# Half of the attention keys projected by seven-product blocks, in the stage of the queries

## The chip, the cores and the metric

The kernel runs on one core of a Trainium2 chip. The metric is the device time of one execution in microseconds (us). PE is the matrix engine, DVE the vector engine, ACT the scalar engine, POOL the general engine, SP the engine that issues most DMAs.

## What is computed

One decoder block over 1024 tokens of width 1024 in float32: an RMSNorm with a modulation gives `h`; one wide projection of `h` gives the operands of a retention branch, of an attention branch and two gates; their sum goes through an output projection, and an MLP follows. The change lies in the attention branch:

```python
proj = h @ w_in                                   # split into parts
for gi, (win, dil) in enumerate(ATT_GROUPS):      # (128,1), (512,4), (2048,16)
    aq, ak, av = parts[4 + 3 * gi], parts[5 + 3 * gi], parts[6 + 3 * gi]
    o, lse = dilated_group(heads(aq, 4), heads(ak, 4), heads(av, 4), tab, win, dil)
# in dilated_group, per head and block of a strided subsequence:
s = q @ k.T * dh ** -0.5 + bias ; mx = max(s) ; e = exp(s - mx) ; o = (e / sum(e)) @ v
```

There are three groups of four heads with 128 channels each, so twelve queries, twelve keys and twelve values. The three groups' outputs of a head are weighted by a softmax over their denominators.

## The kernel before, in words

**Numbers.** Every operand of a matmul is split into a high half (a rounded copy, made by ACT) and a low half (the rest, made by a DVE subtraction). `mm3` (L215) then issues three matmuls, low x high, high x low and high x high, at L219, L221 and L223.

**Stages.** In order: start-up and the first values, the remaining values of attention (`av_blocks`), queries and keys (`queries_keys`, L1186), the values of retention, 32 chunks of retention, attention in two passes (`pair` 0 and 1, each with two heads of each of the three groups), the output of both branches, the MLP.

**Projections of two kinds.** A plain projection of 128 columns is `proj_gen` (L508): eight pieces over the contraction, each six matmuls of 512 columns, so 48. It wants its weights split (`wsplit`, `split_w`). The other kind takes two 128-column projections at once as a 2 x 2 block product done by seven products instead of eight (class `Blocks`): each product has 4 x 3 matmuls, so 84 matmuls for what two plain projections do in 96. The seven products are listed in `ORDER`; `prep` makes DVE's sums of weight blocks and the two halves, `post` combines results on DVE and ACT, and `a_out` (L1136) puts them into token order and stores them to DRAM. `PAIRS` (L1110) lists what the stage `queries_keys` makes in this way: eight pairs of retention's queries and keys ("r"), four of its gates ("s"), six of attention's queries ("a"), four of the output gates ("g"): 22 pairs. Weights of pair q+2 are fetched at the start of pair q, 512 KB twice.

**Attention.** `combos` lists the six heads of a pass in the order group 1, group 1, group 2, group 2, group 0, group 0. `att_step(pair, i)` (L1769) does the plain projection of key i, woven with the scores of head i-1: `weave` puts the scores' matmuls between the eight pieces, the first of them after three pieces (`lag=2`). Step 0 has no scores; in pass 0 it ends the retention and in pass 1 it runs beside the PV part of pass 0. `cover_step(pair, 0)` (L1809) does the same with the projection of an output gate and the scores of head 5. `cover_step(pair, 1)` projects another gate while the softmax ends. From `cover_step(pair, 2)` on, transposes (L1653) and PV products run, woven with further gates.

Of a head i, PE makes the scores bank by bank (three banks for group 1, two for group 2, four for group 0; PSUM has four such banks for them). DVE adds the bias from PSUM into `P` (L1508, L1512), `k_split` (L1473) makes the next key's halves from PSUM (ACT L1477, DVE L1478), `scores_end` (L1515) takes row maxima on DVE (L1518 to L1526), negates them (L1528) and has ACT do eight exponentials (L1531). After head 5, `weights` (L1601) makes the softmax over groups and `pscale` (L1632) scales the probabilities.

**Order.** Engines get their instructions in the order of the program. `Steps.run` (L71) decides where the preparation of a step's operands stands: ahead of a step's body it calls `prepare` for the next step, and for the one after that as far as its first weight:

```python
for t in (s + 1, s + 2):
    ...
        prepare(t, room - done, t == s + 2)
...
body(*args)
```

The operands come through three raw tiles of 512 KB. Whenever one is prepared, the load of the operand three places later is issued on SP. `q_prep` (L1464) makes a query's halves: ACT L1468, DVE L1469; `split_w` a weight's: ACT L209, DVE L210.

Of the kernel before, what the change touches and what calls it, by code (L numbers as in the profile page):

```python
# [11 lines left out]
F32 = mybir.dt.float32  # L12
# [5 lines left out]
P = 128  # L18
D = 1024
S = 1024  # L20
NK = D // P
H = 4
# [111 lines left out]
def block_kernel(ctx, tc, io, stop=None, dbg=None):  # L134
# [25 lines left out]
    def ps_mm(name):  # L160
        return PS["first"].pop("mm", None) or PS["p"].tile([P, 2, 512], F32, tag="mm", bufs=PS["mm"], name=name)
# [346 lines left out]
    def proj_gen(ps, w):  # L508
        for k in range(NK):
            proj_mm(ps, w, [k])  # L510
            yield
# [334 lines left out]
    def wsplit(ap):  # L846
        return ap, split_w


    va_d = [dram.tile([S, 512], F32, name=f"vad{g}") for g in range(3)]  # L850
    aq_d = {(p, g, a): dram.tile([P, S], F32, name=f"aqd{p}{g}{a}") for p in range(2) for g in range(3) for a in range(2)}
    h12_d = [dram.tile([P, 2, 512], F32, name=f"h12d{m}") for m in range(4)]
    av = {}

# [252 lines left out]
    a_pairs = [("a", g, p) for p in range(2) for g in range(3)]  # L1107
    g_pairs = [("g", i) for i in range(len(GATES) // 2)]
    s_pairs = [("s", h) for h in range(H)]
    PAIRS = [{"r": r_pairs, "a": a_pairs, "g": g_pairs, "s": s_pairs}[i].pop(0) for i in "rsrarsrarsrarsraggagga"]  # L1110
    NA = len(PAIRS)
    OA = {}

    def a_load(q, part):
        pair = PAIRS[q]
        src = io[{"g": "w_gate2", "a": "w_aq", "s": "w_rg2"}.get(pair[0]) or f"w_r{pair[1]}"]
        i = 2 * pair[1] + pair[2] if pair[0] == "a" else pair[-1]
        if q == 0 or q % 2 == 0 and part == 2:
            r = x4(f"wa{q}{part}")
        else:  # L1120
            r = wraw.tile([P, 1024], F32, tag="raw", name=f"wa{q}{part}")
        nc.sync.dma_start(r, src[2 * i + part - 1])
        BA.raw[q, part] = r
# [12 lines left out]
    def a_out(q, n, x, y=None):  # L1136

        pair = PAIRS[q]
        if q not in OA:
            OA[q] = [x4(f"qa{q}{i}") for i in range(2)]  # L1140
        i, t = int(n[0]) - 1, int(n[1]) - 1
        o, view = OA[q][i][:, 512 * t:512 * t + 512], lambda z: z
        if pair[0] == "a" and pair[1] == 1:
            o = OA[q][i].rearrange("p (r n i) -> p r n i", r=4, n=2)[:, :, t, :]
            view = lambda z: z.rearrange("p (i r) -> p r i", r=4)
        elif pair[0] == "a" and pair[1] == 2:
            o = OA[q][i].rearrange("p (r i) -> p r i", r=8)[:, :, 64 * t:64 * t + 64]
            view = lambda z: z.rearrange("p (i r) -> p r i", r=8)
        f = {"g": AF.Sigmoid, "s": AF.Silu}.get(pair[0], AF.Copy)
        if y is None:  # L1150
            nc.scalar.activation(o, view(x), f)
        else:
            (nc.vector.tensor_add if n == "12" else nc.vector.tensor_sub)(o, view(x), view(y))
            if pair[0] in "gs":
                nc.scalar.activation(o, o, f)
        if n in ("12", "21"):
            if pair[0] == "g":
                dst = gate_d[GATES[2 * pair[1] + i]]
            elif pair[0] == "s":
                dst = srg_d[pair[1]][i]  # L1160
            elif pair[0] == "a":
                dst = aq_d[pair[2], pair[1], i]
            else:
                return
            nc.sync.dma_start(dst, OA[q][i])
# [203 lines left out]
    steps.add(av_blocks, manual=True)  # L1369
    steps.add(queries_keys, manual=True)  # L1370

    r_loads = {(0, 0): [io["w_rg"][0]], (H - 1, 7): [io["w_ak"][4]]}
    for t in range(1, 2 * H):
        r_loads[(t // 2, 2) if t % 2 else (t // 2 - 1, 7)] = [io["w_rg"][t]]

# [88 lines left out]
    def q_prep(pair, g, a):  # L1464

        def prep(raw):
            hi, lo = ring(f"qh{pair}{g}{a}"), ring(f"ql{pair}{g}{a}")
            nc.scalar.mul(hi, raw, QSCALE)  # L1468
            nc.vector.scalar_tensor_tensor(lo, raw, QSCALE, fv(hi), op0=ALU.mult, op1=ALU.subtract)  # L1469
            A["q", g, a] = (hi, lo)  # L1470
        return prep

    def k_split(pair, g, a, ps):  # L1473
# [76 lines left out]
    def v_fetch(pair, g):  # L1550

        for j in range(2):
            lo = A["l", g, j] = v_tile(pair, g, j, "vl")
            nc.sync.dma_start(fv(lo).rearrange("p (a b) -> p a b", a=4), v_rows(pair, g, j))
# [211 lines left out]

    combos = [(g, a) for g in (1, 2, 0) for a in range(2)]

    def att_step(pair, i):  # L1769

        g, a = combos[i]

        def body(*args):
            ps = ps_mm(f"ak{pair}{i}")
            gen = proj_gen(ps, hd.pop("w") if i == pair == 0 else args[-1])
            if i == len(combos) - 2:
                v_fetch(pair, 0)
            if i > 0:
                last = combos[i - 1]
                weave(gen, NK, scores_gen(pair, *last), len(SB[last[0]]), lag=2)  # L1780
            elif pair == 0:
                args[0](1, True)
                for _ in range(4):
                    next(gen)
                on_T(H - 1, NC - 2)
                on_T(H - 1, NC - 1)
                drain(gen)
                u_final(H - 1)
                for add in result_sums(slice(4, 8)):
                    add()  # L1790
                open_att()
                args[0](3)
            else:
                weave_pv(gen, NK, 0, 10, args[0], lambda: k_split(pair, g, a, ps))
            if i == 0:
                A["st"] = A["p"].tile([P, 3, 8, 4], F32, tag="st", name=f"st{pair}")
                bias_load(pair)
            later_loads()
            if i == 0 and pair == 1:
                banks_sc()  # L1800
            else:
                k_split(pair, g, a, ps)
            if i > 0:
                scores_end(pair, *last)
                if last[1] == 1:
                    stats_out(pair, last[0])
        return body

    def cover_step(pair, n):  # L1809


        i = COVER[pair][n]

        def body(*args):
            if n == 2:
                banks_pv((("mm", "ac2", "ac3", "s", "ac0", "ac1"), ("ac0", "ac1", "s", "ac2", "ac3", "mm"))[pair])
                v_fetch(pair, 2)
            ps = ps_mm(f"gate0{i}")
            gen = proj_gen(ps, args[-1])
            if n == 0:  # L1820
                v_fetch(pair, 1)
                weave(gen, 6, scores_gen(pair, *combos[-1]), len(SB[0]), lag=2, rest=False)
                drain(gen)
                later_loads()
                for j in range(2):
                    vs_high(pair, 0, j)
                t = ring(f"g0{i}s", F32)
                nc.scalar.copy(t, flat(ps))
                A["gate", 0] = t, t
                scores_end(pair, *combos[-1])  # L1830
                weights(pair)
                pscale(0, 0)
            elif n == 1:
                drain(gen)
                t = ring(f"g0{i}s", F32)
                nc.vector.tensor_copy(t, flat(ps))
                A["gate", 1] = t, t
            else:
                weave_pv(gen, NK, pair, 20 if pair else (16, 14)[n - 2], args[0])
                t = A["r1"].tile([P, S], F32, tag="att", bufs=8, name=f"g0{i}s")  # L1840
                nc.scalar.activation(t, flat(ps), AF.Sigmoid)
                nc.sync.dma_start(gate_d[i], t)
        return body

    for pair in range(2):
        for i, (g, a) in enumerate(combos):
            steps.add(att_step(pair, i),
                      ([] if i == pair == 0 else [wsplit(io["w_ak"][g * 4 + 2 * pair + a])]) +
                      ([(aq_d[pair, *combos[i - 1]], q_prep(pair, *combos[i - 1]))] if i > 0 else []),
                      manual=i == 0)  # L1850
        for n in range(len(COVER[pair])):
            more = [(aq_d[pair, *combos[-1]], q_prep(pair, *combos[-1]))] if n == 0 else []
            steps.add(cover_step(pair, n), more + [wsplit(io["w_gate"][len(COVER[0]) * pair + n])], manual=n > 0)


    G = {}
# [779 lines left out]
def _cols(w):  # L2636

    k, n = w.shape
    return np.ascontiguousarray(w.reshape(k // P, P, n // P, P).transpose(2, 1, 0, 3)).reshape(n // P, P, -1)
# [74 lines left out]
def pack(x, c, w_ada, b_ada, norm1_g, w_in, rel_bias, ret_gn_g, ret_gn_b,  # L2714
         w_ret_out, w_att_out, w_o, norm2_g, w_ff1, w_ff2, norm_f_g):
    A = np.asarray
    w = A(w_in)[0]
    att = w[:, 6144:10752].reshape(1024, 3, 3, 512)
    rg = w[:, 4096:6144].reshape(1024, 4, 512)
    gates = lambda js: np.concatenate([w[:, 10752 + P * j:10752 + P * j + P] for j in js], axis=1)  # L2720
    a = {
# [11 lines left out]
        "w_rg": _cols(rg[:, :, :256].reshape(1024, 1024)),  # L2733
        "w_rg2": _pairs(rg[:, :, 256:].reshape(1024, 1024)),
        "w_aq": _pairs(att[:, :, 0].reshape(1024, 1536)),
        "w_ak": _cols(att[:, :, 1].reshape(1024, 1536)),
        "w_av": _vcols(att[:, :, 2].reshape(1024, 1536), 512),
        "w_gate": _cols(gates(i for c in COVER for i in c)),
        "w_gate2": _pairs(gates(GATES)),
# [26 lines left out]
```

## Time and profile before

| | us |
|---|---|
| median of 3 runs | 2184.3 (2184.2 to 2186.07) |
| the profiled execution | 2182.82 |
| its span | 2181.1 |
| PE busy | 2147.4 |
| DVE busy | 1479.0 |
| ACT busy | 947.1 |

The stage of queries lies at about 150 to 570 us of the span, attention's scores of pass 0 at 954 to 1037 us, those of pass 1 at 1107 to 1190 us. In a timeline a row has the start, the duration, the engine, the line, the operation, the output and inputs, and, where the engine idled before, for how long and what ended it. `x3` merges three neighbours.

### The profile page before, as it was taken

What the parts mean: (1) busy time and instruction counts of PE and PEld (TensorE: products, weight loads), DVE (VectorE), ACT (ScalarE), POOL (GpSimd) and SP (SyncE); (2) the same over time, 40 slices, a digit from 0 to 9 for tenths busy, and PEclk for the clock granted to TensorE, in tenths of its full rate; (3) what the DMA queues carried; (4) which work ended last, traced back from release to release, by engine and by line L of the source; (5) the groups of instructions that cost most, each with busy time, mean ns of one, the idle gap of its engine ahead of it and who ended that gap; (6) DMA issues with size and microseconds to landing.
All of it is one profiled execution on the core that took longest, in us unless ns stands there. A gap on an engine that the chain in (4) does not pass through costs nothing.

```text
span 2181.1 us, 27045 instructions
## 1 busy us (share of the span) xinstructions
PE 2147.4 (98%) x10034; PEld 1784.6 (82%) x10034; DVE 1479.0 (68%) x2281; ACT 947.1 (43%) x1715; POOL 178.4 (8%) x192
## 2 busy tenths in 40 slices
PE   7999999999999999999999999999999999999998
PEld 5888888888888888888888888888878888788887
DVE  6756777767566678854655644677876665887855
ACT  4533322333334566654644525434554455433412
POOL 0101111100000334410000000001000000000003
PEclk9999999999999999999999999999999999999999
DMA  9869998734687758977323366653054445645322
GB/s 382 231 193 297 289 328 266 217 136 155 223 297 287 257 181 242 263 222 186 105 81 108 98 250 210 224 184 130 35 202 159 154 143 188 240 138 173 109 87 78
DMA packets 161891, 422.55 MB, mean 194 GB/s; under 512 B 27734, under 2 KB 55645, under 8 KB 157662
## 3 DMA queue, kind: packets, MB, share of 16 engines
q1 hardware_dynamic: 151902, 372.57, 48.4%
q0 software_dynamic: 9856, 48.24, 10.1%
q8 instruction: 79, 1.29, 0.2%
q14 instruction: 54, 0.44, 0.1%
HBM read 325.71 MB, written 160.32 MB: 223 GB/s over the span
## 4 chain that ended last, share of the span: by engine, by line
PE 90%; DVE 4%; ACT 2%; DMA 1%; issue 1%; POOL 0%; SPq 0%; POOLq 0%; DVEq 0%; ACTq 0%
PE qap L219 6%; PE qap L223 6%; PE qap L221 6%; PE fp L219 4%; PE fp L223 4%; PE fp L221 4%; PE ak L219 2%; PE ak L221 2%; PE ak L223 2%; PE f2a L221 2%; PE f2a L223 2%; PE f2a L219 2%; PE rg L221 1%; PE rg L219 1%; PE rg L223 1%; PE va L221 1%
## 5 line engine op out<-in xcount | busy, mean ns | idle before, releaser
L219 PE MATMUL qap<-hh,qaw 128*128 128x512 f32 x264 | 102.8, 389 | 0.1
L221 PE MATMUL qap<-hl,qaw 128*128 128x512 f32 x264 | 102.7, 389 | 0.0
L223 PE MATMUL qap<-hh,qaw 128*128 128x512 f32 x264 | 102.7, 389 | 0.0
L656 POOL TENSOR_TENSOR j<-qk,j 128x512 fp32r<-128x512 f32 x32 | 48.3, 1513 | 311.7 <-ACT j L655 311.7
L2117 POOL TENSOR_TENSOR accnf<-accnf,sqnf 128x256 f32<-128x256 f32 (+1 forms) x18 | 16.6, 921 | 613.2 <-ACT sqnf L2116 613.2
L2221 ACT ACTIVATE a<-a 128x512 f32<-128x512 f32 x48 | 30.3, 632 | 78.0 <-DVE a L2220 78.0
L219 PEld LDWEIGHTS qap<-hh,qaw 128*128 128x128 f32 x264 | 49.6, 188 | 10.8 <-DVE qat L310 0.5
L221 PEld LDWEIGHTS qap<-hl,qaw 128*128 128x128 f32 x264 | 49.5, 188 | 10.3
L223 PEld LDWEIGHTS qap<-hh,qaw 128*128 128x128 f32 x264 | 49.6, 188 | 10.3
L2410 ACT CAST w2h<-w2s 128x512 fp32r<-128x512 f32 x36 | 22.4, 621 | 78.2 <-DVE w2s L2448 78.2
L2117 POOL TENSOR_TENSOR accn<-accn,sqn 128x512 f32<-128x512 f32 x12 | 15.5, 1294 | 496.0 <-ACT sqn L2116 496.0
L276 DVE TENSOR_TENSOR fw<-w1r,fw 128x512 fp32r<-128x512 f32 x48 | 32.9, 688 | 33.2 <-ACT fw L266 33.2
L1531 ACT ACTIVATE P<-P,ng 128x128 f32<-128x128 f32 (+1 forms) x96 | 41.9, 438 | 29.5 <-DVE ng L1528 29.5
L276 DVE TENSOR_TENSOR qaw<-wa,qaw 128x512 fp32r<-128x512 f32 x66 | 45.0, 686 | 11.1 <-ACT qaw L266 11.1
L1309 DVE SCALAR_TENSOR_TENSOR cossin<-cossin,cb 128x1024 f32<-128x1024 f32 x32 | 39.0, 1220 | 16.4 <-DMA cossin<-in_w_ada_dram 16.4
L219 PE MATMUL fp<-h2h,fw 128*128 128x512 f32 x128 | 50.0, 390 | 0.0
L1955 DVE TENSOR_TENSOR rwl<-rwl,rwh 128x1024 fp32r<-128x1024 f32 x25 | 30.2, 1221 | 29.0 <-ACT rwh L1985 29.0
L221 PE MATMUL fp<-h2l,fw 128*128 128x512 f32 x128 | 49.8, 389 | 0.0
L223 PE MATMUL fp<-h2h,fw 128*128 128x512 f32 x128 | 49.8, 389 | 0.0
L219 PE MATMUL roa<-rh,rwl 128*128 128x512 f32 x128 | 49.8, 389 | 0.0
L221 PE MATMUL roa<-rl,rwh 128*128 128x512 f32 x128 | 49.8, 389 | 0.0
L223 PE MATMUL roa<-rh,rwh 128*128 128x512 f32 x128 | 49.8, 389 | 0.0
(3093 smaller groups left out, 7138.1 us busy)
## 6 DMA issues: line engine op xcount, KB each, us to landing
cossin<-in_w_ada_dram SPq DMA_DIRECT2D x32, 512.0 KB, 5.3
v<-vd SPq DMA_DIRECT2D x32, 512.0 KB, 5.7
w1r<-in_w_ff_dram SPq DMA_DIRECT2D x32, 512.0 KB, 4.8
vd<-vo SPq DMA_DIRECT2D x24, 512.0 KB, 6.3
xsd<-as SPq DMA_DIRECT2D x24, 512.0 KB, 2.8
w2r<-in_w_ff2s_dram SPq DMA_DIRECT2D x24, 512.0 KB, 7.6
em<-in_w_ada_dram SPq DMA_DIRECT2D x16, 512.0 KB, 10.2
wrvs<-in_w_rv_dram POOLq DMA_DIRECT2D x16, 512.0 KB, 11.1
```

The costliest lines, as they stand in the source:

```text
L219: nc.tensor.matmul(o, wl, xh, start=first, stop=False, skip_group_check=skip)
L221: nc.tensor.matmul(o, wh, xl, start=False, stop=False, skip_group_check=skip)
L223: nc.tensor.matmul(o, wh, xh, start=False, stop=last, skip_group_check=skip)
L276: nc.vector.tensor_sub(t[:, 512:], src, fv(t[:, :512]))
L656: nc.gpsimd.tensor_sub(t[:, 1], src, fv(t[:, 0]))
L1309: nc.vector.scalar_tensor_tensor(t, t, 1.0, cb, op0=ALU.mult, op1=ALU.mult, accum_out=mods[:, j:j + 1])
L1531: nc.scalar.activation(v, v, AF.Exp, bias=ng[:, blk:blk + 1], accum_out=st[:, g, blk, 2 + a:3 + a])
L1955: nc.vector.tensor_sub(lo, fv(lo), fv(hi))
L2117: (nc.vector if f == 7 else nc.gpsimd).tensor_add(G["acc", key], G["acc", key], sq)
L2221: nc.scalar.activation(o, o, AF.Relu)
L2410: nc.scalar.copy(hi, src)
```

## The change

In each group, the keys of the second head of each pass (six of twelve) are no longer projected in attention. Three new pairs "k", one for each group, are added to `PAIRS`, which has 25 then; `a_out` orders them by token as it does queries, and stores them to `ak_d` in DRAM. In attention they are read back by `k_prep` like a query. The six other keys keep their plain projections: one is now spread over two heads' scores, four pieces to each, with the first scores after two pieces (`lag=1`). The step of head 5's gate is cut into two steps in the same way ("s" and 0). What the body of a step does after its scores, and `Steps.run`, are as before.

```diff
-    PAIRS = [{"r": r_pairs, "a": a_pairs, "g": g_pairs, "s": s_pairs}[i].pop(0) for i in "rsrarsrarsrarsraggagga"]
+    k_pairs = [("k", g) for g in range(3)]
+    PAIRS = [{"r": r_pairs, "a": a_pairs, "g": g_pairs, "s": s_pairs, "k": k_pairs}[i].pop(0)
+             for i in "rsrarsrarsrarsrakggakggak"]
...
+            elif pair[0] == "k":
+                dst = ak_d[i, pair[1]]
...
+    def k_prep(pair, g, a):
+
+        def prep(raw):
+            hi, lo = ring(f"kh{pair}{g}{a}"), ring(f"kl{pair}{g}{a}")
+            nc.scalar.copy(hi, raw)
+            nc.vector.tensor_sub(lo, raw, fv(hi))
+            A["k", g, a] = (hi, lo)
+        return prep
...
+    def weave_scores(pair, i):
+
+        weave(itertools.islice(A["gen"], NK // 2), NK // 2, scores_gen(pair, *combos[i]), len(SB[combos[i][0]]), lag=1)
+
+    def scored(pair, i):
+        scores_end(pair, *combos[i])
+        if combos[i][1] == 1:
+            stats_out(pair, combos[i][0])
+
+    def att_step(pair, i):
+
+        g, a = combos[i + 2 - i % 2]
+
+        def body(*args):
+            if i % 2 == 0:
+                A["ps"] = ps_mm(f"ak{pair}{i}")
+                A["gen"] = proj_gen(A["ps"], args[-1])
+            if i == 2:
+                v_fetch(pair, 0)
+            weave_scores(pair, i)
+            later_loads()
+            if i % 2:
+                drain(A["gen"])
+                k_split(pair, g, a, A["ps"])
+            scored(pair, i)
+        return body
...
+    def rows_load(pair, i):
+        c = combos[i]
+        k = [(ak_d[pair, c[0]], k_prep(pair, *c))] if c[1] else []
+        return k + [(aq_d[pair, *c], q_prep(pair, *c))]
...
+        steps.add(att_first(pair), k_load(combos[0][0], pair) if pair else [], manual=True)
+        for i in range(len(combos) - 2):
+            steps.add(att_step(pair, i), (k_load(combos[i + 2][0], pair) if i % 2 == 0 else []) + rows_load(pair, i))
+        for n in ("s", *range(len(COVER[pair]))):
+            more = rows_load(pair, len(combos) - 2 + (n == 0)) if n in ("s", 0) else []
+            w = [wsplit(io["w_gate"][len(COVER[0]) * pair + (0 if n == "s" else n)])] if n != 0 else []
+            steps.add(cover_step(pair, n), w + more, manual=n not in ("s", 0))
```

`att_first` is the old step 0 under a new name.

More of the change, by code (lines that the diff above doesn't have):

```diff
@@ L851, in block_kernel @@
     aq_d = {(p, g, a): dram.tile([P, S], F32, name=f"aqd{p}{g}{a}") for p in range(2) for g in range(3) for a in range(2)}
+    ak_d = {(p, g): dram.tile([P, S], F32, name=f"akd{p}{g}") for p in range(2) for g in range(3)}
     h12_d = [dram.tile([P, 2, 512], F32, name=f"h12d{m}") for m in range(4)]
@@ L1115, in a_load @@
         pair = PAIRS[q]
-        src = io[{"g": "w_gate2", "a": "w_aq", "s": "w_rg2"}.get(pair[0]) or f"w_r{pair[1]}"]
+        src = io[{"g": "w_gate2", "a": "w_aq", "k": "w_ak2", "s": "w_rg2"}.get(pair[0]) or f"w_r{pair[1]}"]
         i = 2 * pair[1] + pair[2] if pair[0] == "a" else pair[-1]
@@ L1142, in a_out @@
         o, view = OA[q][i][:, 512 * t:512 * t + 512], lambda z: z
-        if pair[0] == "a" and pair[1] == 1:
+        if pair[0] in "ak" and pair[1] == 1:
             o = OA[q][i].rearrange("p (r n i) -> p r n i", r=4, n=2)[:, :, t, :]
             view = lambda z: z.rearrange("p (i r) -> p r i", r=4)
-        elif pair[0] == "a" and pair[1] == 2:
+        elif pair[0] in "ak" and pair[1] == 2:
             o = OA[q][i].rearrange("p (r i) -> p r i", r=8)[:, :, 64 * t:64 * t + 64]
@@ L1370, in block_kernel @@
     steps.add(queries_keys, manual=True)
-    r_loads = {(0, 0): [io["w_rg"][0]], (H - 1, 7): [io["w_ak"][4]]}
+    r_loads = {(0, 0): [io["w_rg"][0]], (H - 1, 7): [io["w_ak"][2]]}
     for t in range(1, 2 * H):
@@ L1767, in block_kernel, with att_first @@
     combos = [(g, a) for g in (1, 2, 0) for a in range(2)]
-    def att_step(pair, i):
-        g, a = combos[i]
+    def att_first(pair):
+        g, a = combos[0]
         def body(*args):
[L1774 to L1781, printed above, removed]
+            ps = ps_mm(f"ak{pair}0")
+            gen = proj_gen(ps, args[-1] if pair else hd.pop("w"))
+            if pair == 0:
                 args[0](1, True)
@@ L1794, in body @@
                 weave_pv(gen, NK, 0, 10, args[0], lambda: k_split(pair, g, a, ps))
-            if i == 0:
-                A["st"] = A["p"].tile([P, 3, 8, 4], F32, tag="st", name=f"st{pair}")
-                bias_load(pair)
+            A["st"] = A["p"].tile([P, 3, 8, 4], F32, tag="st", name=f"st{pair}")
+            bias_load(pair)
             later_loads()
-            if i == 0 and pair == 1:
+            if pair == 1:
                 banks_sc()
@@ L1802, in body @@
                 k_split(pair, g, a, ps)
[L1803 to L1806, printed above, removed]
+        return body
[19 more added lines that the diff above has]
+            scored(pair, i)
         return body
     def cover_step(pair, n):
-        i = COVER[pair][n]
+        i = COVER[pair][n if n != "s" else 0]
         def body(*args):
+            if n == "s":
+                A["ps"] = ps_mm(f"gate0{i}")
+                A["gen"] = proj_gen(A["ps"], args[-1])
+                weave_scores(pair, len(combos) - 2)
+                later_loads()
+                scored(pair, len(combos) - 2)
+                return
             if n == 2:
@@ L1817, in body @@
                 v_fetch(pair, 2)
-            ps = ps_mm(f"gate0{i}")
-            gen = proj_gen(ps, args[-1])
+            ps = A["ps"] if n == 0 else ps_mm(f"gate0{i}")
+            gen = A["gen"] if n == 0 else proj_gen(ps, args[-1])
             if n == 0:
                 v_fetch(pair, 1)
-                weave(gen, 6, scores_gen(pair, *combos[-1]), len(SB[0]), lag=2, rest=False)
+                weave_scores(pair, len(combos) - 1)
                 drain(gen)
@@ L1843, in cover_step, with k_load @@
         return body
-    for pair in range(2):
[L1846 to L1853, printed above, removed]
+    def rows_load(pair, i):
+        c = combos[i]
+        k = [(ak_d[pair, c[0]], k_prep(pair, *c))] if c[1] else []
+        return k + [(aq_d[pair, *c], q_prep(pair, *c))]
+    def k_load(g, pair):
+        return [wsplit(io["w_ak"][2 * g + pair])]
+    for pair in range(2):
+        steps.add(att_first(pair), k_load(combos[0][0], pair) if pair else [], manual=True)
[5 more added lines that the diff above has]
+            steps.add(cover_step(pair, n), w + more, manual=n not in ("s", 0))
     G = {}
@@ L2718, in pack @@
     att = w[:, 6144:10752].reshape(1024, 3, 3, 512)
+    ak = att[:, :, 1].reshape(1024, 3, 2, 2, P)
     rg = w[:, 4096:6144].reshape(1024, 4, 512)
@@ L2735, in pack @@
         "w_aq": _pairs(att[:, :, 0].reshape(1024, 1536)),
-        "w_ak": _cols(att[:, :, 1].reshape(1024, 1536)),
+        "w_ak": _cols(ak[..., 0, :].reshape(1024, 768)),
+        "w_ak2": _pairs(ak[..., 1, :].reshape(1024, 768)),
         "w_av": _vcols(att[:, :, 2].reshape(1024, 1536), 512),
```

## The prediction, made before the result was known

> **What bounds the kernel now.** I read the page first, then the windows over the stage of attention, then the timelines of PE, DVE and ACT in it.
>
> ```profile
> PE 2147.4 (98%) x10034; PEld 1784.6 (82%) x10034; DVE 1479.0 (68%) x2281; ACT 947.1 (43%) x1715; POOL 178.4 (8%) x192
> ```
>
> ```profile
> 980.50:994.10 13.60, 13.60 (x73) 11.61 (x73) 7.07 (x10) 6.52 (x19) 0.00 (x0) 1.00 0.81 220
> ```
>
> PE is busy for 98% of the span, and for all of the 13.60 us of a scores step. DVE and ACT work about half of that step (7.07 and 6.52 us). So PE work that goes is time won, as long as DVE and ACT can follow. What PE work costs is read from starts, since the durations overlap:
>
> ```profile
> 968.07 0.62 PE L219 MATMUL ak<-hh,raw_7985l 128*128 128x512 f32 x2
> ...
> 981.83 0.62 PE L219 MATMUL ak<-hh,raw_8146l 128*128 128x512 f32 x2
> ...
> 1036.87 0.62 PE L219 MATMUL gate<-hh,raw_8495l 128*128 128x512 f32 x2
> ...
> 1047.76 0.60 PE L1653 MATMUL sf<-ct,P 128*128 128x128 f32 x4
> ...
> 1200.37 0.60 PE L1653 MATMUL sf<-ct,P 128*128 128x128 f32 x4
> ```
>
> From 1036.87 to 1047.76 PE does one projection of 48 products with nothing woven in: 10.89 us, 0.227 us a product. From 968.07 to 981.83 it does one projection with one head's scores: 13.76 us, so the scores are 2.87 us. The last two rows are the first transposes of the two head pairs' PV part, to which I measure.
>
> The busy shares hide an order. In the program each step first issues the ACT and DVE halves of the preparation of *later* operands, then the bias additions of its own scores, then the row maxima and the exponentials. Each engine works its list in order. DVE's list:
>
> ```profile
> 966.73 1.89 DVE L1508 TENSOR_TENSOR P<-sc,bias 128x512 f32<-128x512 f32 x3 [2.86 <-DMA bias<-biasd]
> ...
> 977.11 1.23 DVE L1469 SCALAR_TENSOR_TENSOR ql<-raw,qh 128x1024 fp32r<-128x1024 f32 x1 [4.64 <-ACT qh L1468]
> 978.25 1.22 DVE L210 TENSOR_TENSOR raw_8170l<-raw,raw_8170h 128x1024 fp32r<-128x1024 f32 x1
> 979.39 1.88 DVE L1508 TENSOR_TENSOR P<-sc,bias 128x512 f32<-128x512 f32 x3
> 983.13 1.22 DVE L1478 TENSOR_TENSOR kl<-ak,kh 128x1024 fp32r<-128x1024 f32 x1 [1.86 <-ACT kh L1477]
> 984.27 0.68 DVE L1523 TENSOR_REDUCE st<-P 128x4 f32<-128x512 f32 x1
> ...
> 993.20 1.28 DVE L1508 TENSOR_TENSOR P<-sc,bias 128x512 f32<-128x512 f32 x2
> ...
> 997.97 1.21 DVE L1526 TENSOR_REDUCE st<-P 128x8 f32<-128x1024 f32 x1
> ...
> 1020.69 1.88 DVE L1508 TENSOR_TENSOR P<-sc,bias 128x512 f32<-128x512 f32 x3
> ...
> 1033.97 1.88 DVE L1508 TENSOR_TENSOR P<-sc,bias 128x512 f32<-128x512 f32 x3
> 1035.77 0.61 DVE L1512 TENSOR_TENSOR P<-sc,bias 128x256 f32<-128x256 f32 x2
> 1036.41 0.29 DVE L1518 TENSOR_REDUCE st<-P 128x1 f32<-128x128 f32 x1
> ...
> 1038.66 0.17 DVE L1528 TENSOR_SCALAR ng<-st 128x8 f32<-128x8 f32 x1
> ...
> 1044.25 1.33 DVE L1637 TENSOR_SCALAR P<-P,wt 128x128 f32<-128x128 f32 x5
> ...
> 1114.77 0.69 DVE L1508 TENSOR_TENSOR P<-sf,bias 128x512 f32<-128x512 f32 x1
> ```
>
> And ACT's, where an exponential row stands for the first of eight:
>
> ```profile
> 986.31 0.40 ACT L1531 ACTIVATE P<-P,ng 128x128 f32<-128x128 f32 x1 [3.22 <-DVE ng L1528]
> ...
> 989.84 1.04 ACT L1468 ACTIVATE qh<-raw 128x1024 fp32r<-128x1024 f32 x1
> ...
> 999.42 0.40 ACT L1531 ACTIVATE P<-P,ng 128x128 f32<-128x128 f32 x1 [2.62 <-DVE ng L1528]
> ...
> 1002.52 1.05 ACT L1468 ACTIVATE qh<-raw 128x1024 fp32r<-128x1024 f32 x1
> ...
> 1016.20 1.04 ACT L1468 ACTIVATE qh<-raw 128x1024 fp32r<-128x1024 f32 x1
> ...
> 1027.91 0.41 ACT L1531 ACTIVATE P<-P,ng 128x128 f32<-128x128 f32 x1 [3.62 <-DVE ng L1528]
> ...
> 1031.77 1.03 ACT L209 CAST raw_8600h<-raw 128x1024 fp32r<-128x1024 f32 x1
> ```
>
> Look at 977.11 to 979.39: the additions (L1508) stand behind the low halves `ql` and `raw_8170l` and follow them with no idle time, so it is not PE that they waited for. Those low halves wait for ACT's `qh`, which stands behind the eight exponentials of the head before, which wait for its maxima, which wait for its additions. This is a closed ring DVE, ACT, DVE with one turn per head. Today a turn fits into 13.76 us: the row at 983.13 has DVE idle for 1.86 us until the projection is done (<-ACT kh, itself behind PE). PE, not the ring, sets the step.
>
> **The change, part by part.**
>
> *Added in the stage of queries:* three pairs of key heads, seven products each, every one with 12 matmuls, and with them three more rounds of sums, high and low halves, results, two weight loads and two 512 KB stores.
>
> ```profile
> L309 DVE TENSOR_TENSOR qat<-qat,qap x22: 679/687/689, 160.3 to 560.5; 128x512 f32<-128x512 f32 x22
> ```
>
> The 22 pairs start their `s2` result at even steps: (560.5 - 160.3) / 21 = 19.06 us a pair. PE is never short of work there, and the attention pairs among them have the same DVE, ACT and store work as the new ones; that cover is why I price it at PE time alone. If it went, `prep` would be late for the next product, and I have no row of that. Cost: 3 x 19.06 = **+57.2 us**.
>
> *Removed from attention:* three of six projections for each head pair, 6 x 10.89 = 65.3 us of PE. If PE stayed the bound, the change would be 57.2 - 65.3 = -8.1 us. That is what 36 saved matmuls are worth.
>
> *Moved:* each remaining projection is spread over two heads' scores, so PE's step becomes 10.89 / 2 + 2.87 = 8.3 us. Now the ring is the question. A turn is unchanged in its parts: `q` is still prepared for every head; half of the weight splits go, but each is replaced by the ACT copy and DVE subtraction of a key read back. By the order of `prepare`, the preparation bursts are 1, 3, 1, 3, 1 operands: ahead of head 1's additions q2; ahead of head 2's k3, q3 and a weight; then q4; then k5, q5 and a weight; then a weight. (I number the heads 0 to 5: two of group 1, two of group 2, two of group 0.) Prices:
> - additions 1033.97 to 1035.77 = 1.80 (three banks, group 1), 1.20 for two (group 2), to 1036.41 = 2.44 (group 0)
> - low half of a projected key, only at heads 1 and 3: 983.13 to 984.27 = 1.14
> - maxima until the first exponential: 984.27 to 986.31 = 2.04; 997.97 to 999.42 = 1.45; for group 0 the two reductions and the negation, 1036.41 to 1038.66+0.17 = 2.42, with the step to ACT 2.46
> - eight exponentials: 986.31 to 989.84 = 3.53; 999.42 to 1002.52 = 3.10; 1027.91 to 1031.77 = 3.86
> - one operand, from the end of the exponentials to the next additions: 1031.77 to 1033.97 = 2.20; three operands: 1016.20 to 1020.69 = 4.49
>
> Turns: head 0: 1.80+2.04+3.53+2.20 = 9.57. Head 1: 1.80+1.14+2.04+3.53+4.49 = 13.00. Head 2: 1.20+1.45+3.10+2.20 = 7.95. Head 3: 1.20+1.14+1.45+3.10+4.49 = 11.38. Head 4: 2.44+2.46+3.86+2.20 = 10.96. Head 5, from its additions to the scaled probabilities that the first transposes read: 1033.97 to 1044.25+1.33 = 11.61. Together **64.5 us**. Two neighbours average 11.3, 9.7 and 11.3 us, all above PE's 8.3: the ring takes over.
>
> The ring starts where it does today. In pair 0 head 0's additions wait for the bias tile until 966.73, a DMA whose place in SP's queue does not move; in pair 1 they follow three preparations, at 1114.77. So the first transposes come at 966.73 + 64.5 = 1031.2 instead of 1047.76 (16.6 us earlier), and at 1114.77 + 64.5 = 1179.3 instead of 1200.37 (21.1 us earlier, in today's time): **-37.7 us** of the 65.3 that PE gave up.
>
> Does PE ever make the ring wait? Head 2's scores need the low half ready at 966.73+9.57+1.80+1.14 = 979.2; they take some 4 us, and their additions come at 989.3. Head 4's low half is ready at 966.73+30.52+1.20+1.14 = 999.6, its scores then take 2.87 and two woven pieces of projection 2.73, and its additions come at 966.73+41.90 = 1008.6. So no, with 3.4 us to spare. The shorter lead (two pieces of projection instead of three ahead of a head's first scores) costs PE 10.89 / 8 = 1.4 us at most each time, inside the same slack. PE gives back 65.3 - 37.7 = 27.6 us in waits. They land ahead of the scores of heads 2 and 4 (on the low half of their keys), of head 5 (on the four PSUM banks), and at the first transposes: head 5's scores get a bank at 1008.6 + 0.7, take 5.6, the next projection 10.89, which ends at 1025.8; PE then waits 5.4 us for 1031.2.
>
> Queues: SP issues as many loads in the stage as before (three keys for three weights a pair). Each load of the ring of three raw tiles is issued when the operand three places ahead is split:
>
> ```profile
> DMA to landing us min/median/max: 3.5/3.7/10.8
> ```
>
> The tightest, q4, is issued when k3's low half is done, at 966.73+22.57-2.28 = 987.0, and read after head 2's exponentials, at 989.3+1.20+1.45+3.10 = 995.1. The 8.1 us cover the median landing of 3.7, not the longest of 10.8: between 0 and 2.7 us, I take 0, as the median row has it.
>
> *A cost the rows can only bound:* PE's clock after a wait of 5.4 us.
>
> ```profile
> 2170.00:2175.00 5.00, 1.91 (x14) 1.43 (x12) 2.45 (x7) 0.83 (x2) 1.43 (x2) 0.94 0.37 121
> 2175.00:2181.00 6.00, 0.00 (x0) 0.00 (x0) 2.83 (x8) 0.00 (x0) 0.00 (x0) 0.50 0.62 203
> ```
>
> ```profile
> 19.42 2.07 PE L397 MATMUL n10rb<-ct,n1rs 128*128 128x128 f32 x8 [8.34 <-POOL n1rs L390]
> 21.28 1.92 PE L397 MATMUL n11rb<-ct,n1rs 128*128 128x128 f32 x8
> 23.09 3.16 PE L870 MATMUL av<-raw_301h,hh 128*128 128x512 f32 x8
> ```
>
> When PE runs dry at the end its granted clock falls to 0.50. At the start, after an 8.34 us wait, eight products of 512 columns take 3.16 us (0.4 each, not 0.227), so PE is at half speed from 19.42 to about 26.3, 7 us. A slowed first stretch of PV would cost between 0 and half of that, 3.5 us a pair. I take 0, since the waits here are shorter than that one, and keep 7.0 for the range.
> The Trainium skill ("TensorE: Matmul & The Clock Gate", Part 1: The HAM clock gate) says that one idle window of about 3.4 us halves the clock, and a busy one of the same length restores it: an estimate by that is 1.7 us a pair, 3.4 us in all, and 2207 us. The fall to 0.50 in the last rows agrees with it.
>
> **Sum:** 57.2 - 37.7 = +19.5 us; 2182.8 (profiled execution; its span is 2181.1) + 19.5 = 2202.3. The median of the runs is 1.5 us above that execution, so **2204 us**, 0.9% slower.
>
> **Rivals.**
> - *PE stays the bound (faster).* At the additions of heads 1 to 5: had they not to queue behind the next operands, or did a turn cost under 8.3 us, all 65.3 us would come back: 2184.3 - 8.1 = 2176 us. For it: busy sums, DVE and ACT at half of a step. Against: 979.39 behind 978.25. It decides if two turns take less than 16.6 us; I get 19.3 to 22.6. Chance 0.08, of which 0.02 for a mixture near 2184.
> - *The ring and the clock.* As forecast, with PE slowed after its waits: up to 2204 + 7 = 2211; beyond the 3.4 us of slack it would also delay head 4's additions. Chance 0.20.
> - *The ring and a late read-back.* q4 or its like lands late in pair 0, where the DMA share is 0.81 in the window shown: 2204 + 2.7 = 2207. Chance 0.07.
>
> The forecast itself has 0.65. Its own error: 0.2 us on each of 12 turns' terms and some tenths a pair in the queries, +-5. So the range is 2197 to 2211, leaving out the first rival and tails. A measurement of this kernel tells about 0.2% (4.4 us) from no change; so faster 0.06, same 0.02, slower 0.92.
>
> **What would show it.** In the changed kernel's DVE timeline: additions directly behind two or more low halves with no idle time owed to PE; 64 to 65 us from head 0's additions to the first transposes; PE idle ahead of scores for a key's low half (`kl`) and 5 us ahead of the first transposes; 25 starts at 19.06 us in queries. Wrong: additions owed to PE (`<-PE sc`), PE full throughout the scores, or a pair of queries over 19.3 us.

## The result and the profile after

The changed kernel takes 2207.77 us (median of 4 runs, 2205.36 to 2210.05) against 2184.31: 1.0108 times as long, 95% interval 1.0096 to 1.0120, so 1.1% slower. Forecast was 2204. The profiled execution took 2205.36 us (span 2203.6; 22.5 more than before).

Page of the kernel after, busy times:

```profile
PE 2152.1 (98%) x9998; PEld 1786.7 (81%) x9998; DVE 1504.8 (68%) x2323; ACT 956.8 (43%) x1736; POOL 177.2 (8%) x192
```

PE has 36 matmuls fewer and is busy 4.7 us longer. A busy sum does not say at which clock it was earned; how far the clock matters is part of what follows. Now the stage of queries and the stretch of pass 0, in the same views as before. First the groups by line, then DVE's timeline:

```profile
L309 DVE TENSOR_TENSOR qat<-qat,qap x25: 681/689/689, 160.4 to 618.1; 128x512 f32<-128x512 f32 x25
```

```profile
1023.85 1.89 DVE L1522 TENSOR_TENSOR P<-sc,bias 128x512 f32<-128x512 f32 x3 [2.78 <-DMA bias<-biasd]
...
1032.43 1.23 DVE L1474 SCALAR_TENSOR_TENSOR ql<-raw,qh 128x1024 fp32r<-128x1024 f32 x1 [4.64 <-ACT qh L1473]
1033.58 1.88 DVE L1522 TENSOR_TENSOR P<-sc,bias 128x512 f32<-128x512 f32 x3
1035.38 1.21 DVE L1492 TENSOR_TENSOR kl<-ak,kh 128x1024 fp32r<-128x1024 f32 x1
...
1043.13 1.23 DVE L1483 TENSOR_TENSOR kl<-raw,kh 128x1024 fp32r<-128x1024 f32 x1 [4.62 <-ACT kh L1482]
1044.27 1.22 DVE L1474 SCALAR_TENSOR_TENSOR ql<-raw,qh 128x1024 fp32r<-128x1024 f32 x1
1045.41 1.22 DVE L210 TENSOR_TENSOR raw_8646l<-raw,raw_8646h 128x1024 fp32r<-128x1024 f32 x1
1046.55 1.28 DVE L1522 TENSOR_TENSOR P<-sc,bias 128x512 f32<-128x512 f32 x2
...
1054.65 1.28 DVE L1522 TENSOR_TENSOR P<-sc,bias 128x512 f32<-128x512 f32 x2
```

Read the additions (L1522): each after the first, which waits for the bias tile, follows a burst of low halves without idle time, and no wait is owed to PE's scores. In neither pass does a row of DVE or ACT behind those first additions, up to the first transposes, wait for a transfer. The bursts are one operand (1032.43) and three (1043.13 to 1045.41), as worked out. The idle time ahead of a burst ends with ACT, whose halves stand behind the eight exponentials. That is the ring.

PE has become the engine that waits (waits of PE in attention; columns: total us, times, longest):

```profile
PE sc L221 <- DVE kl L1492: 7.2, 5, 2.5
PE sf L1667 <- DVE P L1651: 6.9, 2, 4.1
PE sc L219 <- DVE ql L1474: 3.5, 4, 1.1
PE sc L219 <- DVE P L1522: 1.2, 1, 1.2
```

Last, PE's timeline at the first transposes of pass 0 and of pass 1 (its last row), and the windows there and around head 2's scores (in a window: its length, then the busy time of PE, weight loads, DVE, ACT and POOL; the last three columns are granted clock, DMA share and GB/s):

```profile
1087.66 1.09 PE L1667 MATMUL sf<-ct,P 128*128 128x128 f32 x4 [4.07 <-DVE P L1651]
1088.54 1.06 PE L1667 MATMUL pt000(2, 1, 2)_9169<-ct,P 128*128 128x128 f32 x4
...
1092.12 1.05 PE L221 MATMUL mmf<-hl,raw_8890h 128*128 128x512 f32 x2
...
1095.35 0.63 PE L221 MATMUL mmf<-hl,raw_8890h 128*128 128x512 f32 x2
...
1220.75 1.09 PE L1667 MATMUL sf<-ct,P 128*128 128x128 f32 x4 [2.79 <-DVE P L1651]
```

```profile
1034.00:1038.00 4.00, 1.46 (x8) 1.36 (x7) 4.00 (x6) 0.00 (x0) 1.35 (x2) 0.73 0.70 172
1038.00:1042.00 4.00, 4.00 (x14) 3.42 (x14) 0.48 (x2) 3.45 (x16) 0.00 (x0) 0.50 0.95 195
...
1086.00:1090.00 4.00, 1.94 (x8) 1.57 (x8) 3.90 (x16) 2.25 (x5) 0.00 (x0) 0.63 0.24 4
1090.00:1094.00 4.00, 3.65 (x12) 3.07 (x13) 2.81 (x8) 3.90 (x7) 0.00 (x0) 0.51 0.53 32
1094.00:1098.00 4.00, 4.00 (x31) 3.70 (x30) 0.56 (x1) 1.83 (x4) 0.00 (x0) 1.00 0.60 108
...
1222.00:1226.00 4.00, 3.25 (x12) 2.52 (x11) 3.90 (x9) 3.64 (x7) 0.00 (x0) 0.50 0.43 24
```

After the wait of 4.07 us a pair of such products takes 1.05 us, and 0.63 three microseconds later: the granted clock is 0.51 from 1090 to 1094 us and 1.00 in the window behind. After the wait of 2.79 us in pass 1 it is 0.50.

With these marks the whole difference falls into five stretches (starts of the first addition of a pass, of its first transposes, and of the first product of the branches' output). The last column is the kernel of the final experiment, in its last row the difference from the kernel before:

| us | before | after | difference | predicted | last kernel |
|---|---|---|---|---|---|
| to pass 0's additions | 966.73 | 1023.85 | +57.12 | +57.2 | 1023.28 |
| additions to transposes, pass 0 | 81.03 | 63.81 | -17.22 | -16.6 | 52.79 |
| transposes to pass 1's additions | 67.01 | 69.28 | +2.27 | 0 | 65.92 |
| additions to transposes, pass 1 | 85.60 | 63.81 | -21.79 | -21.1 | 53.88 |
| transposes to the output `ao` | 48.15 | 50.37 | +2.22 | 0 | 48.10 |
| sum | | | +22.6 | +19.5 | -4.6 |

So the two terms with a sure price came as worked out, and what is missing lies in the two stretches that begin with the wait of 4.07 us and its twin of pass 1 (2.79 us).

### The profile page after: what moved, and what is told of

Read it like the earlier page. It is cut to its first block, busy times and chain, and to the rows that moved or that the text cites. A ratio compares the mean times of both kernels' runs of the same rounds, so it can differ in the third digit from the quotient of the medians.

```text
span 2203.6 us, 27076 instructions
## 1 busy us (share of the span) xinstructions
PE 2152.1 (98%) x9998; PEld 1786.7 (81%) x9998; DVE 1504.8 (68%) x2323; ACT 956.8 (43%) x1736; POOL 177.2 (8%) x192
## 4 chain that ended last, share of the span: by engine, by line
PE 84%; DVE 7%; ACT 4%; DMA 2%; issue 1%; SPq 0%; POOL 0%; POOLq 0%; DVEq 0%; ACTq 0%
PE qap L219 7%; PE qap L223 7%; PE qap L221 7%; PE fp L219 4%; PE fp L221 4%; PE fp L223 4%; PE f2a L221 2%; PE f2a L223 2%; PE f2a L219 2%; ACT P L1545 2%; PE rg L221 1%; PE rg L219 1%; PE rg L223 1%; PE va L219 1%; PE va L221 1%; PE va L223 1%
## 5 line engine op out<-in xcount | busy, mean ns | idle before, releaser
L219 PE MATMUL qap<-hh,qaw 128*128 128x512 f32 x300 | 116.8, 389 | 0.3 <-DVE qat L310 0.3
L221 PE MATMUL qap<-hl,qaw 128*128 128x512 f32 x300 | 116.7, 389 | 0.0
L223 PE MATMUL qap<-hh,qaw 128*128 128x512 f32 x300 | 116.7, 389 | 0.0
L1545 ACT ACTIVATE P<-P,ng 128x128 f32<-128x128 f32 (+1 forms) x96 | 41.9, 438 | 57.8 <-DVE ng L1542 57.8
L276 DVE TENSOR_TENSOR qaw<-wa,qaw 128x512 fp32r<-128x512 f32 x75 | 51.2, 687 | 22.4 <-ACT qaw L266 22.4
L219 PEld LDWEIGHTS qap<-hh,qaw 128*128 128x128 f32 x300 | 56.3, 188 | 12.5 <-DVE qat L310 0.8
L2162 POOL TENSOR_TENSOR accnf<-accnf,sqnf 128x256 f32<-128x256 f32 (+1 forms) x18 | 16.6, 922 | 612.7 <-ACT sqnf L2161 612.7
L221 PEld LDWEIGHTS qap<-hl,qaw 128*128 128x128 f32 x300 | 56.3, 188 | 11.7
L223 PEld LDWEIGHTS qap<-hh,qaw 128*128 128x128 f32 x300 | 56.3, 188 | 11.7
L266 ACT CAST qaw<-wa 128x512 fp32r<-128x512 f32 x75 | 45.2, 616 | 34.4 <-PE qap L223 24.3
```

What stands on the lines that cost most here:

```text
L219: nc.tensor.matmul(o, wl, xh, start=first, stop=False, skip_group_check=skip)
L221: nc.tensor.matmul(o, wh, xl, start=False, stop=False, skip_group_check=skip)
L223: nc.tensor.matmul(o, wh, xh, start=False, stop=last, skip_group_check=skip)
L266: nc.scalar.copy(t[:, :512], src)
L276: nc.vector.tensor_sub(t[:, 512:], src, fv(t[:, :512]))
L1545: nc.scalar.activation(v, v, AF.Exp, bias=ng[:, blk:blk + 1], accum_out=st[:, g, blk, 2 + a:3 + a])
```

## The experiments

The theory: a ring of DVE and ACT, one turn a head, sets attention's pace, because the preparation of later operands stands between the exponentials and the next additions. Rivals: PE is still the bound; late read-backs or the transfers around them hold DVE and ACT; PE's halved clock explains more than the ring does.

**1. One ACT copy more per head, in both kernels.** It stands between the maxima and the exponentials and writes what it reads.

```diff
+        nc.scalar.copy(t[:, :1024], t[:, :1024])
         ng = p.tile([P, 8], F32, tag="ng", bufs=2,
```

In the kernel after:

> The changed kernel with one more ACT copy of 128x1024 per head, in place, between the maxima and the exponentials (twelve copies, results unchanged). If the ring of DVE and ACT sets the scores' pace, each copy lengthens its turn by its own 0.95 us and about 0.1 us of handing over: +11 to +13 us on the changed kernel's 2207.8, so about 2220. If PE, the read-back loads or the shorter lead set it, ACT has idle time for twelve copies: 0 to +2 us, at most 2210.

In the kernel before:

> The same twelve copies in the kernel before. By the ring theory a turn there has 1.86 us of room (DVE waits for the projection) and the end of a pass 2.4 us, so the copies vanish: 0 to +1 us on 2184.3. If the number of ACT instructions mattered by itself, +11 to +13 us as in the changed kernel.

After: 2218.47 us (2216.89 to 2220.3), ratio 1.016 (1.0145 to 1.0175), 10.7 more than without the copy (2207.77; 13.3 more than its repetition of experiment 3), where I expected 11 to 13. Before: 2184.11 against 2183.80, ratio 1.0003 (0.9993 to 1.0013). Rows of ACT in the kernel after with the copy:

```profile
1027.38 1.05 ACT L1541 COPY P<-P 128x1024 f32<-128x1024 f32 x1 [7.66 <-DVE st L1538]
1028.45 1.28 ACT L1546 ACT_TABLE_LOAD   x1
...
1040.26 1.04 ACT L1541 COPY P<-P 128x1024 f32<-128x1024 f32 x1 [5.05 <-DVE st L1538]
```

The turns of pass 0 grew from 9.73, 12.97, 8.10, 11.35, 10.96 to 11.88, 13.85, 8.98, 12.22, 11.83, and head 5's part from 11.60 to 12.47: five by 0.87 or 0.88, the first by 2.15 (a table load stands in it). In the kernel before, the two stretches from additions to transposes take 81.26 and 85.61 us with the copies, 81.03 and 85.60 without. The same microsecond of ACT is free before and is paid in every head after. This settles that the bound has moved to the ring.

**2. Each side of the change alone.** The three key pairs made and stored, but attention as before:

```diff
-    PAIRS = [... for i in "rsrarsrarsrarsraggagga"]
+    PAIRS = [... for i in "rsrarsrarsrarsrakggakggak"]
```

> The kernel before with the three added pairs in the stage of queries alone: six key projections are made by seven products and stored, and nobody reads them. Priced at PE time: 3 x 19.06 = +57.2 us on 2184.3, so 2241.5 (2240.5 to 2243). If sums and halves on DVE and ACT or the stores held PE up, more than 2244.

And attention as after, without the pairs. The stored queries are read in place of the keys, so its numbers are others; loads and instructions are the same:

```diff
-        k = [(ak_d[pair, c[0]], k_prep(pair, *c))]
+        k = [(aq_d[pair, *c], k_prep(pair, *c))]
```

> The changed kernel without the three added pairs; in place of the six keys it reads the stored queries back (so its scores are of other numbers). Ring and clock: the changed kernel's 2207.8 less 57.2, so 2150.6 (2148 to 2153). If the two parts disturb each other, for instance through DMA traffic, the sum of both parts' differences from the kernel before is more than 2 us off the whole change's +23.5.

The queries alone: 2241.17 us, +57.8, ratio 1.0263 (1.0247 to 1.0278). Attention alone: 2152.19, -31.2, ratio 0.9858 (0.9843 to 0.9873), with turns of 9.72, 12.98, 8.10, 11.35, 10.95. Each sign and size is right. Their sum is +26.5 where the whole change costs 21.7 to 23.5, so it misses by 3 to 5 us, more than the 2 that I allowed; two medians of the kernel after differ by 2.6 us (2207.77, and 2205.17 in experiment 3), and that does not cover all of it. Up to the output `ao` the traces of the two parts come to +57.7 and -32.4, together 2.7 more than the whole change. About half of that, 1.3 us, lies in the two stretches behind the transposes of attention alone (70.12 and 50.84 us, where the kernel after has 69.28 and 50.37). The rest stays open.

**3. The lead of the scores, and a repetition.**

```diff
-        weave(..., lag=1)
+        weave(..., lag=2)
```

> The changed kernel with the scores of a head behind three pieces of projection again, as before, instead of two. Ring theory: the lead lies inside PE's slack, 2206 to 2209 us, no change. If the shorter lead to a key's low half were the cost, PE's waits for it (7.2 us in the trace) would mostly go: 2201 to 2204 us.

> The changed kernel itself once more, for the comparison with the filler kernel and the others of this call: 2206 to 2209 us by every theory. With 2208 the filler's 2201.3 is a gain of 6.5 us, twice what its trace shows in attention (3.1 us); with 2204 to 2205 it is the 3.1 us.

2206.44 (ratio 1.0105, 1.0088 to 1.0122) and, for the unchanged kernel after, 2205.17 (ratio 1.0099, 1.0085 to 1.0113). With the longer lead PE waits 5.34 and 5.36 us at the first transposes in place of 4.07 and 2.79. The stretches up to them stay as they were (63.80 and 63.79 us), so the lead is not what holds the scores. The two stretches behind them grow to 70.22 and 50.89 us, so the trace has a price for PE's longer wait, 1.5 us, too small to show in the medians.

**4. PE kept busy through the wait.** Ahead of the gate's projection at the first transposes, 18 (pass 0) and 12 (pass 1) of its matmuls are done once more, into a bank that the projection then overwrites.

```diff
             elif n == 1:
+                for _ in range(3 - pair):
+                    mm3([ps[:, 0, :], ps[:, 1, :]], wk(args[-1], 0), hx[0], True, True)
                 drain(gen)
```

> The changed kernel with 18 (pass 0) and 12 (pass 1) matmuls of 512 columns more, recomputed and overwritten, ahead of the second gate's projection, in the time that PE waits for the first transposes (4.07 and 2.79 us in the trace). If PE's halved clock after that wait costs the 3.1 us that the ring leaves open, PV starts at full clock and the time falls by 2 to 3.5 us although PE does more: about 2205 us. If the 3.1 us have another cause, 0 to +1 us: 2208 to 2209 us.

2201.25 us (2200.6 to 2203.04), ratio 1.0082 (1.0067 to 1.0097): 3.9 to 6.5 us *faster* than the two medians of the kernel after, with 30 matmuls more, and more than the 2 to 3.5 us that I expected. Its slowest run (2203.04) is below the fastest of the eight of the kernel after (2203.51). PE and windows of this kernel:

```profile
1087.87 0.69 PE L1667 MATMUL sf<-ct,P 128*128 128x128 f32 x4
```

```profile
1086.00:1090.00 4.00, 3.00 (x17) 2.13 (x15) 3.73 (x16) 2.69 (x8) 0.00 (x0) 1.00 0.24 4
1090.00:1094.00 4.00, 3.44 (x22) 3.09 (x23) 2.95 (x8) 3.64 (x6) 0.00 (x0) 1.00 0.35 30
```

The transposes come at the same time as before, take 0.69 us in place of 1.09, and the clock stays at 1.00. The two stretches behind them take 67.63 and 48.73 us in place of 69.28 and 50.37: 3.3 us in both together. So the missing 3 us are the halved clock; what the medians gain beyond that these stretches do not explain.

**5. The order of attention changed.** In every step of the scores the preparation stands behind the row maxima and ahead of the exponentials, one step further ahead.

```diff
+            if isinstance(manual, tuple):
+                prepare(s + 1, 3)
+                body(lambda: [prepare(s + t, 3) for t in manual], *args)
...
-    def scores_end(pair, g, a):
+    def scores_end(pair, g, a, late=lambda: None):
...
+        late()
         for blk in range(8):
...
             nc.scalar.activation(v, v, AF.Exp
```

> The changed kernel with the same instructions in another order: what a step prepares for later is moved from ahead of its own bias additions to behind its maxima and ahead of its exponentials, and reaches one step further. That opens the ring. Ring theory: PE takes over again, the scores come at about 8.3 us a head and the whole at 2176 to 2182 us, faster than before. If the late key halves, the read-back or the projections' lead were the cause, nothing or little changes: 2203 to 2210 us.

2186.13 us (2183.76 to 2188.69), ratio 1.001 (1.0001 to 1.0020): 21.6 off the kernel after, 4 more than the upper end of what I expected. DVE in pass 1:

```profile
1169.66 1.22 DVE L213 TENSOR_TENSOR raw_9840l<-raw,raw_9840h 128x1024 fp32r<-128x1024 f32 x1
1170.80 1.22 DVE L1477 SCALAR_TENSOR_TENSOR ql<-raw,qh 128x1024 fp32r<-128x1024 f32 x1
1173.02 0.69 DVE L1525 TENSOR_TENSOR P<-sc,bias 128x512 f32<-128x512 f32 x1 [1.00 <-PE sc L226]
1175.76 0.69 DVE L1525 TENSOR_TENSOR P<-sc,bias 128x512 f32<-128x512 f32 x1 [2.05 <-PE sc L226]
```

Here the additions wait for PE: the ring is open, and from additions to scaled probabilities pass 1 takes 52.95 us in place of 64.7. Pass 0 takes 59.9. ACT shows a wait that could be the cause:

```profile
1037.02 1.06 ACT L1476 ACTIVATE qh<-raw 128x1024 fp32r<-128x1024 f32 x1 [2.81 <-DMA raw<-aqd]
...
1047.38 1.06 ACT L1476 ACTIVATE qh<-raw 128x1024 fp32r<-128x1024 f32 x1 [4.85 <-DMA raw<-aqd]
...
1062.61 1.06 ACT L1476 ACTIVATE qh<-raw 128x1024 fp32r<-128x1024 f32 x1 [9.18 <-DMA raw<-aqd]
```

With the ring gone the read-backs are late. ACT's waits for queries come to 23.2 us in pass 0 (a first one of 6.36 stands ahead of the rows shown) and to 5.0 in pass 1 (3.22, 0.15, 1.61). In pass 0 alone eight 1 MB transfers of retention's results run on POOL's queue.

**6. An edit that moved nothing.** I moved these eight transfers behind attention's scores in the program, in three kernels: the reordered one, the one before and the one after.

```diff
-                for add in result_sums(slice(4, 8)):
-                    add()
+                A["sums"] = result_sums(slice(4, 8))
...
+            if pair == 0 and n in (2, 3):
+                for _ in range(4):
+                    A["sums"].pop(0)()
```

> The kernel with the opened ring (operands prepared behind the maxima, one step further ahead), and besides that the eight DMAs by which POOL sums blocks of the retention's result move from the first step of attention to the PV part of pass 0. In the trace of the opened ring, pass 0 is no longer held by the ring but by read-back loads that take 8 to 13 us behind these sums. Theory: pass 0 then runs at PE's pace as pass 1 does there, 5 to 10 us less than 2186: 2176 to 2181 us, faster than the kernel before. Rival: pass 0 is held by something else, 2184 to 2188.

> The kernel before with the same eight DMAs moved. PE is busy throughout its scores, so nothing is to be won: 0 to -1 us on its time, by every theory. A gain of more than 2 us would say that the gain of the opened ring with moved sums is owed to the move alone.

> The changed kernel with the same eight DMAs moved. Ring theory: no DMA ends a wait inside the ring, so only its start can come sooner (the bias tile, 2.8 us): 0 to -4 us, 2203 to 2208. If late read-back loads were the cause of the loss in pass 0, -8 us or more.

Reordered: 2185.97 (ratio 1.0011, 1.0002 to 1.0020); before: 2182.68 (1.0000, 0.9991 to 1.0008); after: 2205.85 (1.0100, 1.0084 to 1.0115). No change anywhere. POOL's timeline of the reordered kernel shows that the edit did not do what I expected of it:

```profile
1016.11 0.58 POOL L607 DMA_DIRECT2D yt<-y  x1 [16.43 <-DMA y<-on]
1023.78 0.82 POOL L608 DMA_DIRECT2D yt<-y  x1 [7.08 <-DMA yt<-y]
...
1065.74 0.84 POOL L608 DMA_DIRECT2D yt<-y  x1 [6.23 <-DMA yt<-yt]
```

Without the edit the first of them starts at 1015.69 and the last at 1067.96. POOL has nothing else in its list there, and each of its waits ends with a transfer: it issued each as soon as its data were ready, though the program has it later. In the other two kernels the starts stay as well (958.51 to 1010.07 for 958.17 to 1011.74 us before, 1016.16 to 1067.29 for 1015.86 to 1066.31 after). These three runs say nothing of the transfers' effect; that pass 0 took 57.5 us in place of 59.9 can't be put down to a move that did not take place.

**7. The transfers really held back.** In the reordered kernel a POOL subtraction of the softmax weights stands ahead of them.

```diff
+            if pair == 0 and n == 2:
+                w = A["w", 0]
+                hold = A["p"].tile([P, 1], F32, tag="hold", name="hold")
+                nc.gpsimd.tensor_tensor(hold, w[:, 0, 0:1], w[:, 0, 1:2], op=ALU.subtract)
             if pair == 0 and n in (2, 3):
```

> The reordered kernel with the eight 1 MB transfers on POOL's queue really held back in pass 0. Their earlier move in the program did not move them in time: in those three traces POOL, with nothing else to do, issued them from 1016 to 1067 us as before. Here a small POOL subtraction that reads the softmax weights stands ahead of them, so they start after about 1075 us. If the transfers are what makes the read-back operands late in pass 0 of the reordered kernel (59.9 us from head 0's additions to the scaled probabilities, against 52.95 in pass 1), pass 0 falls to 53 to 55 us and the median by 5 to 7 us, to 2178 to 2182. If the loads are late because of SP's own list (V's fetches and the statistics ahead of them), pass 0 stays at 57 to 60 us and the median at 2183 to 2188.

2177.75 us (2175.8 to 2178.73; before 2183.14), ratio 0.9972 (0.9960 to 0.9984): it beats both kernels. POOL, then DVE, of this kernel:

```profile
1073.83 0.28 POOL L1859 TENSOR_TENSOR hold<-wt 128x1 f32<-128x1 f32 x1 [72.17 <-issue]
1074.39 0.61 POOL L607 DMA_DIRECT2D yt<-y  x1 [0.28 <-issue]
```

```profile
1041.11 1.22 DVE L213 TENSOR_TENSOR raw_8630l<-raw,raw_8630h 128x1024 fp32r<-128x1024 f32 x1
1042.25 1.22 DVE L1477 SCALAR_TENSOR_TENSOR ql<-raw,qh 128x1024 fp32r<-128x1024 f32 x1
1044.47 0.69 DVE L1525 TENSOR_TENSOR P<-sc,bias 128x512 f32<-128x512 f32 x1 [1.01 <-PE sc L226]
1047.21 0.69 DVE L1525 TENSOR_TENSOR P<-sc,bias 128x512 f32<-128x512 f32 x1 [2.05 <-PE sc L226]
```

Pass 0 now takes 51.8 us from additions to scaled probabilities, below the 53 to 55 that I expected, and its additions wait for PE as in pass 1. PE is busy at a granted clock of 1.00 for all of the 52.79 and 53.88 us from additions to transposes. ACT's waits for queries in pass 0 fall to 3.71, 0.45 and 0.57 us. The loads' median time to landing, from the groups of transfers between 1010 and 1070 us, without and with the hold:

```profile
raw<-aqd SPq DMA_DIRECT2D x4, 512.0 KB, 7.9
...
raw<-akd SPq DMA_DIRECT2D x2, 512.0 KB, 13.0
```

```profile
raw<-aqd SPq DMA_DIRECT2D x4, 512.0 KB, 5.3
...
raw<-akd SPq DMA_DIRECT2D x2, 512.0 KB, 6.5
```

So the change paid with two things together, an order that leaves the ring open and free queues for the read-backs: that kernel is 5.4 us faster than the one before. Held-back transfers without the new order were not run, in neither kernel. In the kernel after, no wait of the ring ends with a transfer, so a gain there is not to be expected. What of the 5.4 us the kernel before would gain without the change is not shown; from additions to transposes it has little to win, since its PE is busy at a granted clock of 1.00 for all of the 81.03 and 85.60 us.

## Why the prediction was right, and where its sum was short

- *Queries, +57.2.* 24 steps from 160.4 to 618.1 are 19.07 us each; the stage moved attention by 57.12. The cover of DVE, ACT and stores held, also by itself (+57.8).
- *The ring, 64.5 us.* The turns were 9.73, 12.97, 8.10, 11.35 and 10.96, and 11.60 to the scaled probabilities: 64.7 in both passes. The closed list of waits, not the busy shares, gave this; the extra copy and the reordering showed it from both sides.
- *PE's waits, 27.6 us.* The rows show 18.8, at the places named (keys' low halves, the bank of head 5, the transposes at 4.07 and 2.79 for 5.4) and 3.5 of it at a place not named, queries' low halves. About 6 us more went to half clock: by an estimate from windows of 1 us, 3.0 us a pass of clock not granted while PE was busy between additions and transposes (14 matmuls in a 4 us window at 0.50). Some 3 us are not accounted for.
- *The failed step: "a slowed first stretch of PV ... I take 0, since the waits here are shorter than that one".* It measured 2.27 and 2.22 us. The transposes started 0.6 to 0.7 us earlier than my marks had them, being issued on the first scaled block, so 3.1 us net. That is the rival "the ring and the clock", to which I gave 0.20. The Trainium skill ("TensorE: Matmul & The Clock Gate", Part 1: The HAM clock gate) led to an estimate of 1.7 us a pair; the busy PE of experiment 4 recovered 1.65 and 1.64 us in the traces. The trace agrees with that size, but not with a full idle window as the condition: in pass 1 the clock fell at about 1220.2 us, some 2.2 us into the wait of 2.79. I had weighed a single row (8.34 us at the start) above the estimate.
- *The rival "PE stays the bound"*, 8.1 us faster, was wrong for this order of instructions and nearly right for another: with the ring open and the transfers held that kernel is 5.4 us faster than the one before.
- *Late read-backs* cost nothing in the kernel after, whose turns are the same in both passes; they became the next bound in pass 0 as soon as the ring was gone. I had not priced that for the reordered kernel, whence its miss by 4 us.

Of 2207.77 - 2204 = 3.8 us, 3.1 are the clock; the rest is within the 2.6 us by which two medians of the same kernel differ (2205.17 and 2207.77). That the repetition lies only 1.2 us above the forecast is luck: its trace has the same long stretches behind the transposes (69.39 and 50.38 us).

## What to carry to other kernels

Before taking work off an engine that is busy for 98%, follow one turn through the in-order lists of the others and add up its parts: if preparation of later operands stands between an engine's result and the next consumer, the turn is a floor that the busy shares do not show. Price a wait of PE with what it costs behind it, and look whether an idle engine can be given harmless work through it. To move a transfer in time, give it something to wait for; moving its line did nothing here, on a queue that had nothing else to do.

## What the hardware showed that was not expected

- The clock halves without a long single wait. In pass 0 waits of 1.06 and 2.54 us with one product between them (PE busy 1.46 us in the window from 1034 to 1038 us) were followed by a window at 0.50, so a nearly idle stretch was enough. In the reordered kernel (experiment 5) a wait of 1.57 us between pass 0's first transposes, behind one of 0.17, was followed by a clock of 0.51 from 1085.4 to 1088.8 us, while a wait of 1.56 us at the same place in the kernel of experiment 4 left it at 1.00. The length of one wait alone does not decide it.
- Thirty useless matmuls made the kernel faster: 3.3 us in the two stretches behind the waits.
- With eight 1 MB transfers running on POOL's queue, SP's reads of keys took twice as long to land (13.0 us for 6.5, medians of two loads) and those of queries half as long again (7.9 for 5.3, of four).
